# Expert weights in 1 MB transfers of two neighbouring rows per partition, and slot pairs opened oldest first, in a two-layer diffusion transformer with experts

## The chip, the core and the metric

The kernel runs on one core of a Trainium2 chip. The metric is the device time of one execution in microseconds, as the median of several runs.

## What is computed

Two layers over 256 latent and 256 context tokens of width 1024, in float32. Layer 0 mixes the tokens by windowed attention, layer 1 by differential attention; each is followed by a mixture of 32 SwiGLU experts, of which each token uses two. Shift, scale and gate come from a conditioning vector. The part that the change touches, shortened from the reference:

```python
h = rmsnorm(x, norm_g[i, 1]) * (1 + mod[:, 4]) + mod[:, 3]      # mod[:, 3] is the shift
u = xblk @ w_up[e]                                              # w_up[e]: 1024 x 1024
y = (silu(u[:, :512]) * u[:, 512:]) @ w_down[e]                 # w_down[e]: 512 x 1024
out[token] += y * weight[token, e]
```

The experts of layer 0 see all 512 tokens, those of layer 1 the 256 latent ones. Both layers read every expert: 32 x 6.29 MB each, 403 MB of the 484 MB that the kernel reads.

## The kernel before

**Experts.** They are taken in 16 pairs a layer. The two experts of a pair (s = 0, 1) lie side by side in halves of 64 rows or columns, each with room for 64 tokens. For each pair PE gathers the tokens (L1148), transposes them (L1194, in `spread_tokens`, where DVE also adds the shift, L1196), multiplies them with w_up (`up`, L1205: 8 steps of k, 4 matmuls of 128x512 each), ACT and DVE apply the gate (`gate`, L1212 to L1214), PE transposes the result (L1236), multiplies with w_down (`down`, L1248: 4 steps of k), and spreads it back over the tokens (`combine`, L1287). The stages of neighbouring pairs overlap by an order written out by hand: the down matmuls of one pair come right before the up matmuls of the next. The last pair of a layer takes w_down by columns (`down_last`, L1260). A step k uses 128 rows of the weights: k*128 to k*128 + 127, one row on each partition.

**Weights.** All large weights go through one list, `plan`, in a fixed order, by DMAs that SP issues (`Stream.one`, L177), into 43 slots of 4 KB per partition (`Slot`). The list `free` is a queue: a slot that is freed goes to its end and the next use takes its head. A DMA waits until the last reader of its slot is done. Each expert DMA is 512 KB: 128 rows of 4 KB, which follow each other in memory. The same slots hold the split weights and other large values of the attention: `split` (L513, L517) turns a streamed float32 weight into a high and a low part, on ACT and on POOL or DVE, for the projections (L542).

**Around the experts.** `Post` normalizes the tokens after the attention, computes the router's logits and turns the tokens into rows (`flip`; in layer 1 the copies are L921 on ACT). `logit_bias` (L835 to L847) computes what the shift adds to the logits. After the fifth pair a condition decides whether an expert has over 64 tokens; the branch for that isn't taken here (the jump shows at L1081).

```python
        def one(self):                              # Stream
            src, shape = plan[self.pos]
            self.pos += 1
            s = Slot()
            v = s.f(*shape)
            nc.sync.dma_start(v, src)               # L177
            self.ready.append((s, v))
```

Of the kernel before, what the change touches and what calls it, by code (L numbers as in the profile page):

```python
# [18 lines left out]
OP = mybir.AluOpType  # L19
# [37 lines left out]
def _hybrid_dit(ctx, tc, a, out):  # L57
# [5 lines left out]
    places = [[nc.alloc_sbuf_tensor_at(f"slot{c}{i}", [128, 1024], dt, offset=base + 4096 * i).ap()  # L63
               for c, dt in (("f", F32), ("r", F32R))] for i in range(SLOTS)]
    const = ctx.enter_context(tc.tile_pool(name="const", bufs=1))
    pool = ctx.enter_context(tc.tile_pool(name="act", bufs=1))
# [45 lines left out]
    free = list(range(SLOTS))  # L112

    class Slot:
        def __init__(self, recent=False):
            assert free, "no slot left"
            self.s = free.pop(-1 if recent else 0)

# [10 lines left out]
        def free(self):  # L129
            free.append(self.s)  # L130
            self.s = None

    class Ring:
# [29 lines left out]
    class Stream:  # L163
# [23 lines left out]
    def plan_mod(l, third, halves, k):  # L187
        w = a["mod_w"][l, k * 128:(k + 2) * 128]
        for h in halves:
            for q in range(2):  # L190
                c0 = third * 2048 + q * 1024 + h * 512
                plan.append((w[:, c0:c0 + 512].rearrange("(q p) n -> p q n", p=128), (2, 512)))

    def plan_cols(src, c0, ks=range(0, KT, 2)):
        for k in ks:
            plan.append((src[k * 128:(k + 2) * 128, c0:c0 + 512].rearrange("(q p) n -> p q n", p=128), (2, 512)))

    def plan_out(src):
        for n in range(4):
            for k in range(0, KT, 4):  # L200
                plan.append((src[k * 128:(k + 4) * 128, n * 256:(n + 1) * 256].rearrange("(q p) n -> p q n", p=128),
                             (4, 256)))

    def plan_experts(l):
        for p in range(NE // 2):
            for k in range(KT):
                for s in range(2):
                    plan.append((a["moe_w_up"][l, 2 * p + s, k * 128:(k + 1) * 128, :], (1024,)))
            for k in range(4):
                for s in range(2):  # L210
                    w = a["moe_w_down"][l, 2 * p + s]
                    if p + 1 < NE // 2:
                        plan.append((w[k * 128:(k + 1) * 128, :], (1024,)))
                    else:
                        plan.append((w[:, k * 256:(k + 1) * 256].rearrange("(q p) n -> p q n", p=128), (4, 256)))

    late_cols = [(c, h, k) for c in (3, 2, 4, 5) for h in range(2) for k in range(0, KT, 2)]

    def plan_late(n):
        for _ in range(n):  # L220
            c, h, k = late_cols.pop(0)
            c0 = c * 1024 + h * 512
            plan.append((a["mod_w"][1, k * 128:(k + 2) * 128, c0:c0 + 512].rearrange("(q p) n -> p q n", p=128),
                         (2, 512)))

    wq0, wq1 = a["win_w_qkv"][0], a["diff_w_qkv"][0]
    mod_steps = [(m // 3, m % 3, (0, 1), k) for m in range(1, 4) for k in range(0, KT, 2)]
    for d in range(4):
        for k in range(0, KT, 4):
            for q in range(2):  # L230
                c0 = q * 1024 + d * 256
                plan.append((a["mod_w"][0, k * 128:(k + 4) * 128, c0:c0 + 256].rearrange("(q p) n -> p q n", p=128),
                             (4, 256)))
        plan_cols(wq0, 1024, (2 * d,))
# [14 lines left out]
    for k in range(KT):  # L249
        plan.append((a["diff_w_o"][0, k * 128:(k + 1) * 128, :], (1024,)))  # L250
    plan_experts(1)
# [178 lines left out]

    x_slots = [Slot(recent=True) for _ in range(KT // 2)]
    xT = [x_slots[k // 2].f(2, 512)[:, k % 2] for k in range(KT)]
# [400 lines left out]
    v0s.free()  # L833

    def logit_bias(l, nr):  # L835
        ps = bank("G")
        for k in range(KT):
# [11 lines left out]
    def part(v, c0, nt, n):  # L849
        return v[:, c0:c0 + nt * n].rearrange("p (t n) -> p t n", t=nt)  # L850

    class Post:
        def __init__(self, l, nt, lb=None):
# [5 lines left out]
            if nr == 2:  # L859
# [3 lines left out]
                for h in range(2):  # L863
# [5 lines left out]
                    pe.matmul(ps, ones, dg, start=True, stop=True)  # L869
                    se.activation(self.db.f()[:, h * 512:(h + 1) * 512], ps, AF.Copy)  # L870
            self.norm = Norm(self.T, 2 if nr == 2 else 4, ge, tags="s" if nr == 2 else "st")
# [5 lines left out]
            homes[l].slot.free()  # L877
            self.slots = [[Slot() for _ in range(1 if t in WHOLE[l] else 2)] for t in range(nt)]
            self.tok = [[s.r() if len(g) > 1 else s.f() for s in g] for g in self.slots]
# [6 lines left out]
        def scaled(self, k):  # L886
            l = self.l
            if k % 4 == 0:
                self.xs[k // 4] = [Slot() for _ in range(2)]
            xa = self.xs[k // 4][k % 4 // 2].f(2, 512)[:, k % 2, :self.T]  # L890
# [16 lines left out]
        def flip(self, h, tags, ks=range(4)):  # L907
            for t in range(self.nt):
                if ks[0] == 0:
                    self.banks[t] = bank(tags[t])  # L910
                ps = self.banks[t]
                for k in ks:
                    pe.transpose(ps[:, k * 128:(k + 1) * 128], self.xa[4 * h + k][:, t * 128:(t + 1) * 128], ident)
                cs = slice(ks[0] * 128, (ks[-1] + 1) * 128)
                hs = slice(h * 512 + ks[0] * 128, h * 512 + (ks[-1] + 1) * 128)
                if t < 2 and len(self.tok[t]) > 1:
                    hi, lo = (v[:, hs] for v in self.tok[t])
                    se.activation(hi, ps[:, cs], AF.Copy)
                    ve.tensor_tensor(lo, ps[:, cs], hi.bitcast(F32), op=OP.subtract)
                elif self.nr == 1:  # L920
                    se.activation(self.slots[t][-1].f()[:, hs], ps[:, cs], AF.Copy, scale=self.ri[:, t:t + 1])  # L921
                elif t % 2 == 0:
                    se.activation(self.slots[t][-1].f()[:, hs], ps[:, cs], AF.Copy)
                else:
                    ve.tensor_copy(self.slots[t][-1].f()[:, hs], ps[:, cs])
            if ks[-1] == 3:
# [51 lines left out]
    def moe(l, nt, post, after, finish):  # L978
# [77 lines left out]
        for p in range(np_):  # L1056
# [17 lines left out]
            if p == IF_AT:  # L1074
# [116 lines left out]
    def spread_tokens(l, st, h):  # L1191
        ps = bank("G")
        for k in range(4):
            pe.transpose(ps[:, k * 128:(k + 1) * 128], st["x"][h][:, k * 128:(k + 1) * 128], ident)  # L1194
        o = row("t")
        ve.tensor_tensor(o.rearrange("p (k c) -> p k c", k=4), ps.rearrange("p (k c) -> p k c", k=4),  # L1196
                         mods[l][:, 3, 4 * h:4 * h + 4, 0:1].to_broadcast([128, 4, 128]), op=OP.add)
        st["xt"].append(o)

    def up(st, u, k):  # L1200
        w = [stream.next() for _ in range(2)]
        for h in range(2):
            for s in range(2):
                c0 = (k % 4) * 128 + 64 * s
                pe.matmul(u[h][64 * s:64 * s + 64, :], st["xt"][k // 4][:, c0:c0 + 64],  # L1205
                          w[s][1][:, h * 512:(h + 1) * 512], start=(k == 0), stop=(k == KT - 1))
        for s in range(2):
# [33 lines left out]
    def down(acT):  # L1241
        y = [bank("B"), bank("B")]
        for k in range(4):
            w = [stream.next() for _ in range(2)]
            for h in range(2):
                for s in range(2):
                    c0 = k * 128 + 64 * s
                    pe.matmul(y[h][64 * s:64 * s + 64, :], acT[:, c0:c0 + 64],  # L1248
                              w[s][1][:, h * 512:(h + 1) * 512], start=(k == 0), stop=(k == 3))
            for s in range(2):  # L1250
                w[s][0].free()
        return y
# [41 lines left out]
    def overflow(l, nt, key, W, ri, tok, hT):  # L1294
        T = nt * 128
        for t in range(nt):
            for h in range(2):
# [13 lines left out]
                for k in range(4):  # L1311
                    ve.tensor_scalar(hT[4 * h + k][:, t * 128:(t + 1) * 128], ps[:, k * 128:(k + 1) * 128],
                                     mods[l][:, 3, 4 * h + k, 0:1], None, op0=OP.add)
        Wov = row("p", (128, nt, NE))
# [5 lines left out]
        with tc.For_i(0, NE, 1) as i:  # L1320
# [12 lines left out]
            ve.tensor_copy(wrow[:, :T], ps[:, :T])  # L1333
            wu = a["moe_w_up"][l, bass.ds(i, 1)].rearrange("o (k p) n -> p (o k) n", p=128)
            wd = a["moe_w_down"][l, bass.ds(i, 1)].rearrange("o (k p) n -> p (o k) n", p=128)
# [178 lines left out]
    def move_x(after):  # L1514
        slots = [Slot() for _ in range(2)]
        with tc.issue_after(after.ins):
# [270 lines left out]
```

## Time and profile before

| | before |
|---|---|
| median of 3 runs | 1559.56 us (1555.63 to 1561.87) |
| profiled execution | 1559.65 us |
| its span | 1557.9 us |
| granted TensorE clock, mean | 0.974 of 2.4 GHz |
| PE busy | 1459.4 us, 94% |
| DVE, ACT, POOL busy | 44%, 25%, 12% |
| moved by SP's queue | 483.66 MB |

The page counts the busy time of each engine over one profiled execution. PE's matmuls overlap, so a busy PE need not be at its peak; what ends its idle time is told by the views of waits. The kernel has four stretches: layer 0's attention (0 to about 300 us), its experts (to 800), layer 1's attention (to 1065), its experts (to about 1535), and a short end.

### The profile page before, as it was taken

The page shows a single profiled execution, that of the slowest core. Times are in us where ns is not written, and L with a number is a line of the kernel's source. Part 1 is how long each engine was busy: PE and PEld are TensorE (multiplying, and loading weights), DVE is VectorE, ACT ScalarE, POOL GpSimd, SP SyncE. Part 2 cuts the span into 40 slices and gives each one's busy share as a digit, 9 for nine tenths or more (in the row PEclk, how much of TensorE's full clock was granted, in tenths as well). Part 3 has the DMA queues.
Part 4 walks back from the last instruction along what each step waited for, and adds up shares of the span by engine and source line. Part 5 has one row for each costly group of instructions (what it writes and reads, how often), then busy time and mean ns, then how long its engine had stood idle before and what let it go on. Part 6 is the DMA issues. An engine that isn't in the chain of part 4 may idle for free. (4 is left out here: it accounts for less than half of the span.)

```text
span 1557.9 us, 20210 instructions
## 1 busy us (share of the span) xinstructions
PE 1459.4 (94%) x7407; PEld 802.0 (51%) x7407; DVE 692.2 (44%) x1617; ACT 385.2 (25%) x823; POOL 186.2 (12%) x147
## 2 busy tenths in 40 slices
PE   6998999799999999999997889798999899999997
PEld 4765567444444454445445578684434343443444
DVE  3348862533333343334348976863223232332333
ACT  4426652211100111001123236552111110110112
POOL 2314541000000000000014364100000000000000
PEclk9999999799999999999997999998999999999999
DMA  9777225799989999999963842477999999999992
GB/s 329 245 230 250 82 96 194 281 373 399 390 348 393 399 398 386 402 399 399 381 210 95 287 168 81 167 272 279 388 409 409 408 409 409 409 409 409 409 396 73
DMA packets 169696, 485.67 MB, mean 312 GB/s; under 512 B 20826, under 2 KB 41587, under 8 KB 169587
## 3 DMA queue, kind: packets, MB, share of 16 engines
q1 hardware_dynamic: 169088, 483.66, 81.9%
q8 instruction: 63, 1.03, 0.3%
q10 hardware_dynamic: 498, 0.60, 0.1%
q14 instruction: 47, 0.38, 0.1%
HBM read 483.16 MB, written 1.05 MB: 311 GB/s over the span
## 5 line engine op out<-in xcount | busy, mean ns | idle before, releaser
L1205 PE MATMUL ps<-slotf,row 128*64 128x512 f32 x2048 | 450.8, 595 | 2.1 <-DVE row L1196 2.1
L1205 PEld LDWEIGHTS ps<-slotf,row 128*64 128x64 f32 x2048 | 145.6, 137 | 291.1 <-issue 275.3
L1248 PE MATMUL ps<-slotf,row 128*64 128x512 f32 x960 | 212.6, 595 | 0.0
L542 PE MATMUL ps<-slotr,slotr 128*128 128x512 f32 x768 | 193.6, 405 | 9.5 <-DVE slotf L1410 4.2
L505 DVE SCALAR_TENSOR_TENSOR slotf<-ps,mod,slotf 128x256 f32<-128x256 f32 x408 | 167.3, 476 | 62.4 <-PE ps L1287 29.7
L542 PEld LDWEIGHTS ps<-slotr,slotr 128*128 128x128 f32 x768 | 145.1, 194 | 48.2 <-DVE slotf L1410 5.0
L1248 PEld LDWEIGHTS ps<-slotf,row 128*64 128x64 f32 x960 | 66.2, 137 | 124.9 <-issue 118.1
L1213 DVE SCALAR_TENSOR_TENSOR row<-row,ps 128x512 f32<-128x512 f32 x30 | 20.6, 688 | 234.4 <-ACT row L1212 234.4
L1212 ACT ACTIVATE row<-ps 128x512 f32<-128x512 f32 x30 | 17.9, 597 | 427.8 <-PE ps L1205 388.4
L1274 DVE SCALAR_TENSOR_TENSOR row<-ps,ty,row 128x512 fp32r<-128x512 f32 x60 | 45.1, 751 | 176.4 <-ACT row L1273 173.2
L1273 ACT ACTIVATE row<-ps,ty 128x512 fp32r<-128x512 f32 x60 | 41.3, 688 | 262.9 <-PE ps L1248 262.6
L1287 PE MATMUL ps<-row,row 128*128 128x512 f32 (+1 forms) x512 | 104.5, 349 | 1.1 <-DVE slotf L505 1.0
L1287 PEld LDWEIGHTS ps<-row,row 128*128 128x128 f32 x512 | 77.3, 189 | 36.6 <-ACT row L1212 21.1
L517 POOL TENSOR_TENSOR slotr<-slotf,slotr 128x1024 fp32r<-128x1024 f32 x32 | 81.0, 2543 | 90.0 <-ACT slotr L513 62.0
L1196 DVE TENSOR_TENSOR row<-ps,mod 128x512 f32<-128x512 f32 x64 | 42.7, 687 | 102.4 <-PE ps L1194 101.7
L477 POOL TENSOR_TENSOR row<-row,row 128x512 f32<-128x512 f32 (+1 forms) x13 | 15.0, 1157 | 576.0 <-PE ps L1287 519.9
L1148 PE MATMUL ps<-slotf,row 128*128 128x512 f32 x128 | 65.3, 634 | 6.9 <-PEq L1081 4.7
L1148 PE MATMUL ps<-slotr,row 128*128 128x512 f32 x256 | 70.6, 420 | 0.0
L513 ACT ACTIVATE slotr<-slotf 128x1024 fp32r<-128x1024 f32 x44 | 46.0, 1056 | 49.3 <-DMA slotf<-in_diff_w_qkv 22.9
L1148 PEld LDWEIGHTS ps<-slotr,row 128*128 128x128 f32 x256 | 48.1, 198 | 10.0 <-issue 0.8
L1509 DVE SCALAR_TENSOR_TENSOR row<-slotf,keep,row 128x512 f32<-128x512 f32 x42 | 50.6, 1222 | 1.1
L1373 PE MATMUL ps<-slotr,slotr 128*128 128x512 f32 x192 | 47.6, 399 | 0.0
(311 smaller groups left out, 1552.2 us busy)
## 6 DMA issues: line engine op xcount, KB each, us to landing
slotf<-in_moe_w_up SPq DMA_DIRECT2D x512, 512.0 KB, 9.5
slotf<-in_moe_w_down SPq DMA_DIRECT2D x256, 512.0 KB, 10.1
slotf<-in_mod_w SPq DMA_DIRECT2D x96, 512.0 KB, 6.0
slotf<-in_diff_w_qkv SPq DMA_DIRECT2D x24, 512.0 KB, 4.4
slotf<-in_win_w_qkv SPq DMA_DIRECT2D x12, 512.0 KB, 5.1
slotf<-in_win_w_o SPq DMA_DIRECT2D x8, 512.0 KB, 4.1
slotf<-in_diff_w_o SPq DMA_DIRECT2D x8, 512.0 KB, 4.4
slotf<-in_x SPq DMA_DIRECT2D x2, 512.0 KB, 4.0
```

Of the source, the lines that this page charges most:

```text
L505: ve.scalar_tensor_tensor(xT[k][:, sl], ps[:, sl], g[:, k, r:r + 1], xT[k][:, sl], op0=OP.mult, op1=OP.add)
L513: se.activation(hv, v, AF.Copy)
L517: (eng or (ge if split_i[0] % 3 == 0 else ve)).tensor_tensor(lv, v, hv.bitcast(F32), op=OP.subtract)
L542: pe.matmul(ps[t], h[:, x, ts], w[y][:, kk, :], start=(k + kk == 0 and n == 0), stop=(k + kk == KT - 1 and n == 2))
L1148: pe.matmul(g, P[:, t, :] if len(tok[t]) > 1 else P[:, t, :].bitcast(F32), v[:, hs], start=(t == 0 and i == 0), stop=(t == nt - 1 and i == ...
L1196: ve.tensor_tensor(o.rearrange("p (k c) -> p k c", k=4), ps.rearrange("p (k c) -> p k c", k=4), mods[l][:, 3, 4 * h:4 * h + 4, 0:1].to_bro ...
L1205: pe.matmul(u[h][64 * s:64 * s + 64, :], st["xt"][k // 4][:, c0:c0 + 64], w[s][1][:, h * 512:(h + 1) * 512], start=(k == 0), stop=(k == KT ...
L1248: pe.matmul(y[h][64 * s:64 * s + 64, :], acT[:, c0:c0 + 64], w[s][1][:, h * 512:(h + 1) * 512], start=(k == 0), stop=(k == 3))
L1274: ve.scalar_tensor_tensor(yl, y[h], wsl, yh.bitcast(F32), op0=OP.mult, op1=OP.subtract)
L1287: pe.matmul(out, part[:, c * 128:(c + 1) * 128], st["PT"][:, :T], start=(i == 0), stop=(i == 1))
L1373: pe.matmul(ps, w[x][:, k % 4, ms], oT0[k][1][:, y, :], start=(k == 0 and i == 0), stop=(k == KT - 1 and i == 2))
L1509: ve.scalar_tensor_tensor(acc, w[:, kk, :], keep[:, k + kk:k + kk + 1], acc, op0=OP.mult, op1=OP.add)
```

## The change

**What it does.** All expert weights except the last pair's w_down of each layer come in DMAs of 1 MB: two neighbouring rows, 8 KB, on each partition, into two neighbouring slots (`Wide`). For that, partition p holds the rows 8p to 8p + 7 of w_up and 4p to 4p + 3 of w_down, so that the rows which one DMA reads lie 32 KB (w_up) and 16 KB (w_down) apart, and step k uses the rows 8p + k (4p + k).

The tokens' columns and the gate's result have to be in the same order. `flip` deals the tokens' columns out by their remainder (`deal`, `dealt`), `gate` writes its result with a stride of 128 columns, and `turned_shift`, new in `logit_bias`, brings the shift into that order once a layer, with two instructions on PE and five on DVE.

A pair of slots is free when both are; `whole_pairs` lists the free pairs, the one that has been free longest first. Single users take one half of such a pair and keep the other for the next of their kind (`spare`), users of two slots take a pair (`buddies`).

The diff, cut:

```diff
+    def whole_pairs():
+        at = {i: n for n, i in enumerate(free)}
+        found = [(max(at[i], at[i + 1]), i) for i in range(0, SLOTS - 1, 2) if i in at and i + 1 in at]
+        return [i for _, i in sorted(found)]
...
     class Slot:
-        def __init__(self, recent=False):
-            assert free, "no slot left"
-            self.s = free.pop(-1 if recent else 0)
+        def __init__(self, recent=False, at=None, kind=""):
+            if at is None:
+                assert free, "no slot left"
+                at = spare.pop(kind, None)
+                if recent:
+                    at = next((i for i in free[::-1] if i ^ 1 not in free), free[-1])
+                elif at not in free:
+                    pairs = whole_pairs()
+                    if pairs:
+                        at = pairs[0]
+                        spare[kind] = at + 1
+                    else:
+                        at = free[0]
+            free.remove(at)
+            self.s = at
...
+    class Wide:
+        def __init__(self):
+            self.at = whole_pairs()[0]
+            free.remove(self.at)
+            free.remove(self.at + 1)
...
+        def free(self):
+            free.extend((self.at, self.at + 1))
...
-            src, shape = plan[self.pos]
+            src, shape, wide = plan[self.pos]
             self.pos += 1
-            s = Slot()
+            s = Wide() if wide else Slot(kind="stream")
             v = s.f(*shape)
-            nc.sync.dma_start(v, src)
+            nc.sync.dma_start(wide_places[s.at // 2] if wide else v, src)
...
     def plan_experts(l):
         for p in range(NE // 2):
-            for k in range(KT):
+            for j in range(KT // 2):
                 for s in range(2):
-                    plan.append((a["moe_w_up"][l, 2 * p + s, k * 128:(k + 1) * 128, :], (1024,)))
...
+                    w = a["moe_w_up"][l, 2 * p + s].rearrange("(p k) n -> p (k n)", k=KT)
+                    plan.append((w[:, j * 2048:(j + 1) * 2048], (2, 1024), True))
+            if p + 1 < NE // 2:
+                for j in range(2):
+                    for s in range(2):
+                        w = a["moe_w_down"][l, 2 * p + s].rearrange("(p k) n -> p (k n)", k=4)
+                        plan.append((w[:, j * 2048:(j + 1) * 2048], (2, 1024), True))
...
-        hi, lo = Slot(), Slot()
+        hi, lo = buddies()
...
+    def turned_shift(l):
+        work = row("x")
+        mod16 = homes[l].v[:, 964:980]
+        ve.tensor_reduce(mod16, ident.rearrange("p (k a) -> p a k", a=16), axis=AX.X, op=OP.add)
+        row8, t = work[:, 0:128], work[:, 128:256].rearrange("p (b a) -> p b a", b=8)
+        ps = bank("G")
+        pe.transpose(ps[0:8, 0:128], mods[l][:, 3, :, 0], ident)
+        ve.tensor_copy(row8[0:8], ps[0:8, 0:128])
+        ps = bank("G")
+        each = work[0:8, 256:384]
+        ve.tensor_copy(each.rearrange("j (k a) -> j k a", k=8), ident[0:8, 0:8].unsqueeze(2).to_broadcast([8, 8, 16]))
+        pe.matmul(ps[:, 0:128], each, row8[0:8], start=True, stop=True)
+        ve.tensor_tensor(t, ps[:, 0:128].rearrange("p (a b) -> p b a", b=8), mod16[:, None, :].to_broadcast([128, 8, 16]),
+                         op=OP.mult)
...
+        ve.tensor_reduce(moe_shift[l], t, axis=AX.X, op=OP.add)
...
+    def dealt(v, k0, n):
+        return v.rearrange("t (b m) -> t b m", b=8)[:, :, 16 * k0:16 * (k0 + n)]
+
+    def deal(v):
+        return v.rearrange("t (m b) -> t b m", b=8)
...
-                    se.activation(self.slots[t][-1].f()[:, hs], ps[:, cs], AF.Copy, scale=self.ri[:, t:t + 1])
+                    se.activation(raw, src, AF.Copy, scale=self.ri[:, t:t + 1])
...
-                stream.ahead(len(free) - 1)
+                stream.ahead(len(stream.ready) + len(whole_pairs()))
...
-        w = [stream.next() for _ in range(2)]
+        if k % 2 == 0:
+            st["w_up"] = [stream.next() for _ in range(2)]
+        w = st["w_up"]
...
-        for s in range(2):
-            w[s][0].free()
+        if k % 2:
+            for s in range(2):
+                w[s][0].free()
...
-        ve.scalar_tensor_tensor(ac, th, 1.0, u[0], op0=OP.add, op1=OP.mult)
-        ve.scalar_tensor_tensor(ac, ac, 0.5, u[1], op0=OP.mult, op1=OP.mult)
+        ve.scalar_tensor_tensor(th, th, 1.0, u[0], op0=OP.add, op1=OP.mult)
+        ve.scalar_tensor_tensor(ac.rearrange("s (k p) -> s p k", k=4), th.rearrange("s (p k) -> s p k", k=4), 0.5,
+                                u[1].rearrange("s (p k) -> s p k", k=4), op0=OP.mult, op1=OP.mult)
```

**Where instructions move.** On SP, at the change from layer 1's attention to its experts. Before, the queue has the last weights of the attention (in_diff_w_o) mixed with the first w_up:

```order
L177 DMA slotf_99<-in_diff_w_o 128x1024
L177 DMA slotf_77<-in_diff_w_o 128x1024
L177 DMA slotf_97<-in_moe_w_up 128x1024
L177 DMA slotf_135<-in_diff_w_o 128x1024
L177 DMA slotf_111<-in_moe_w_up 128x1024
L177 DMA slotf_91<-in_diff_w_o 128x1024
L177 DMA slotf_63<-in_diff_w_o 128x1024
L177 DMA slotf_81<-in_diff_w_o 128x1024
L177 DMA slotf_65<-in_moe_w_up 128x1024
L177 DMA slotf_125<-in_moe_w_up 128x1024
L177 DMA slotf_67<-in_moe_w_up 128x1024
L177 DMA slotf_99<-in_moe_w_up 128x1024
```

and now:

```order
L216 DMA slotf_119<-in_diff_w_o 128x1024
L216 DMA slotf_97<-in_diff_w_o 128x1024
L216 DMA slotf_95<-in_diff_w_o 128x1024
L216 DMA slotw_149<-in_moe_w_up 128x2048
L216 DMA slotw_143<-in_moe_w_up 128x2048
L216 DMA slotw_161<-in_moe_w_up 128x2048
L216 DMA slotw_147<-in_moe_w_up 128x2048
L216 DMA slotw_155<-in_moe_w_up 128x2048
L216 DMA slotw_152<-in_moe_w_down 128x2048
L216 DMA slotw_159<-in_moe_w_up 128x2048
```

The 512 KB DMAs of one row per partition (128x1024) have become half as many of two (128x2048), and the first of them stands behind the last in_diff_w_o.

On PE, in the attention of layer 1 where `logit_bias` runs (mod is the table of shifts and scales; the 1x36 matmuls are the logits' bias, L838 before, L902 now). Before:

```order
L1580 MATMUL ps_7785<-ident,row_7700 128x128 x4
L1610 MATMUL ps_7791<-ident,slotf_71 128x128 x2
L1560 MATMUL ps_7803<-slotr_94,slotr_108 128x512 x2
L1560 MATMUL ps_7809<-slotr_94,slotr_108 128x512 x2
L838 MATMUL ps_7814<-slotf_117,mod_237 1x36 x8
L844 MATMUL ps_7826<-ty_7823,ident 128x36
L1639 MATMUL ps_7610<-slotf_127,slotf_77 128x256 x2
L1580 MATMUL ps_7832<-ident,slotf_75 128x128 x4
```

and now:

```order
L1660 MATMUL ps_7629<-ident,row_7544 128x128 x4
L1690 MATMUL ps_7635<-ident,slotf_59 128x128 x2
L1640 MATMUL ps_7647<-slotr_138,slotr_82 128x512 x2
L1640 MATMUL ps_7653<-slotr_138,slotr_82 128x512 x2
L887 MATMUL ps_7660<-ident,mod_258 8x128
L892 MATMUL ps_7663<-row_7658 128x128
L902 MATMUL ps_7669<-slotf_61,mod_258 1x36 x8
L908 MATMUL ps_7681<-ty_7678,ident 128x36
L1719 MATMUL ps_7454<-slotf_139,slotf_113 128x256 x2
```

The transpose of the shift (8x128) and the matmul that turns it (128x128) have come in between the projection's matmuls (128x512) and the bias, back to back. In layer 0 the same two stand about a dozen matmuls apart.

## Rows read from the trace of the kernel before

**Rows 1.** The page, busy time of PE and PEld over the whole span (us, share, instructions), and what the DMA engines moved in each of the 40 slices of 38.95 us (GB/s).

```profile
PE 1459.4 (94%) x7407; PEld 802.0 (51%) x7407; DVE 692.2 (44%) x1617; ACT 385.2 (25%) x823; POOL 186.2 (12%) x147
...
GB/s 329 245 230 250 82 96 194 281 373 399 390 348 393 399 398 386 402 399 399 381 210 95 287 168 81 167 272 279 388 409 409 408 409 409 409 409 409 409 396 73
```

**Rows 2.** Busy time of each engine in four stretches: start and end (us), length, each engine's busy us and instructions, granted TensorE clock, share of the DMA engines' time, GB/s. 20:40 is the start of the kernel, 300:800 the experts of layer 0, 800:1065 the attention of layer 1, 1065:1535 its experts.

```profile
20.00:40.00 20.00, 18.44 (x130) 12.87 (x130) 7.41 (x20) 8.92 (x18) 8.29 (x7) 0.91 1.03 330
300.00:800.00 500.00, 493.42 (x2368) 236.60 (x2364) 183.98 (x409) 57.22 (x93) 0.00 (x0) 0.99 0.98 381
800.00:1065.00 265.00, 225.59 (x1146) 178.85 (x1146) 203.10 (x457) 126.46 (x283) 90.30 (x58) 0.94 0.53 184
1065.00:1535.00 470.00, 454.56 (x2159) 192.75 (x2157) 133.31 (x282) 52.33 (x96) 0.00 (x0) 0.99 0.98 387
```

**Rows 3.** The chain of work that ended last, in order of time: start us, us, what. From the down matmuls (L1248) of one pair of layer 1 to those of the next, and the down matmuls of the last pair (L1260).

```profile
1247.92 7.02 PE ps L1248 x32
1254.93 13.73 PE ps L1205 x64
...
1277.11 7.02 PE ps L1248 x32
...
1535.10 3.67 PE ps L1260 x32
...
1543.22 1.88 PE ps L1260 x16
```

**Rows 4.** What PE waited for between 1080 and 1535 us: us in total, times, the longest. These are all its rows.

```profile
PE ps L1194 <- DVE row L1152: 6.7, 15, 0.4
PE ps L1148 <- PEq L1081: 4.7, 1, 4.7
PE ps L1205 <- DVE row L1196: 0.5, 1, 0.5
```

**Rows 5.** The DMA queue of SP in order of time (start us, us, engine, line, operation, out<-in, how many merged): the w_up of two neighbouring pairs of layer 1, and the w_down of its last pair.

```profile
1331.08 19.52 SPq L177 DMA_DIRECT2D slotf<-in_moe_w_up  x16
...
1361.78 19.48 SPq L177 DMA_DIRECT2D slotf<-in_moe_w_up  x16
...
1506.46 13.42 SPq L177 DMA_DIRECT2D slotf<-in_moe_w_down  x8
```

**Rows 6.** DMA issues of the page: how many, KB of each, median us from issue to landing.

```profile
slotf<-in_moe_w_up SPq DMA_DIRECT2D x512, 512.0 KB, 9.5
slotf<-in_moe_w_down SPq DMA_DIRECT2D x256, 512.0 KB, 10.1
```

**Rows 7.** PE in order of time: the first down matmuls of two neighbouring pairs of layer 0.

```profile
418.88 1.51 PE L1248 MATMUL ps<-slotf,row 128*64 128x512 f32 x6
...
450.65 1.94 PE L1248 MATMUL ps<-slotf,row 128*64 128x512 f32 x8
```

**Rows 8.** What SP's queue waited for over the whole span, longest first: us in total, times, longest.

```profile
SPq L177 <- DMA slotf<-in_moe_w_up: 304.2, 357, 2.4
```

**Rows 9.** The instructions of two lines of logit_bias: duration in ns (shortest/median/longest), first and last start.

```profile
L840 DVE COPY ty<-ps x2: 176/180/184, 223.3 to 1009.0; 2x36 f32<-2x36 f32 x1, 1x36 f32<-1x36 f32 x1
...
L844 PE MATMUL ps<-ty,ident x6: 274/274/294, 223.8 to 1009.4; 2*128 2x36 f32 x4, 1*128 1x36 f32 x2
```

**Rows 10.** What PE waited for between 800 and 1080 us, the end of layer 0 and the attention of layer 1: us in total, times, longest.

```profile
PE ps L456 <- DVE row L454: 9.1, 1, 9.1
PE ps L542 <- DVE slotf L1410: 4.2, 2, 3.0
PE ps L1476 <- DVE slotf L1509: 3.3, 2, 2.8
PE ps L585 <- POOL slotf L571: 3.1, 1, 3.1
...
PE ps L542 <- DVE row L569: 1.8, 1, 1.8
...
PE ps L844 <- DVE ty L840: 0.9, 1, 0.9
```

**Rows 11.** Durations as in rows 9: L569 (DVE, a strided form: 16 runs of 16 columns), L563 (DVE, plain) and L921 (ACT, the token copies of layer 1).

```profile
L569 DVE TENSOR_TENSOR row<-ps,slotf x28: 280/415/425, 56.1 to 989.3; 128x256 f32<-128x256 f32 x24, 128x128 f32<-128x128 f32 x4
...
L563 DVE TENSOR_TENSOR slotf<-ps,slotf x7: 425/691/693, 55.8 to 987.5; 128x512 f32<-128x512 f32 x6, 128x256 f32<-128x256 f32 x1
...
L921 ACT ACTIVATE slotf<-ps,ri x4: 680/688/697, 1058.8 to 1060.5; 128x512 f32<-128x512 f32 x4
```

**Rows 12.** All engines in order of time around a gate of layer 1: its second DVE step, and the transposes of its result on PE.

```profile
1117.01 0.69 DVE L1214 SCALAR_TENSOR_TENSOR row<-row,ps 128x512 f32<-128x512 f32 x1
...
1120.25 0.60 PE L1236 MATMUL ps<-ident,row 128*128 128x128 f32 x4
```

**Rows 13.** What the engines waited for between 815 and 945 us, longest first.

```profile
POOL slotr L517 <- ACT slotr L513: 29.5, 8, 8.2
ACT slotr L513 <- DMA slotf<-in_diff_w_qkv: 22.9, 12, 5.1
```

**Rows 14.** What SP's queue waited for between 780 and 1060 us, longest first.

```profile
SPq L177 <- PE ps L542: 49.5, 12, 8.0
SPq L177 <- PE ps L1560: 42.9, 5, 22.9
```

More of the change, by code (lines that the diff above doesn't have):

```diff
@@ L64, in _hybrid_dit @@
                for c, dt in (("f", F32), ("r", F32R))] for i in range(SLOTS)]
+    wide_places = [nc.alloc_sbuf_tensor_at(f"slotw{i}", [128, 2048], F32, offset=base + 8192 * i).ap()
+                   for i in range(SLOTS // 2)]
     const = ctx.enter_context(tc.tile_pool(name="const", bufs=1))
@@ L131, in free, with buddies, f @@
             self.s = None
+    def buddies():
+        at = whole_pairs()
+        if not at:
+            return Slot(), Slot()
+        return Slot(at=at[0]), Slot(at=at[0] + 1)
+    class Wide:
[3 more added lines that the diff above has]
+            free.remove(self.at + 1)
+        def f(self, *shape):
+            return wide_places[self.at // 2].rearrange("p (a b) -> p a b", a=shape[0])
+        def free(self):
+            free.extend((self.at, self.at + 1))
     class Ring:
@@ L249, in _hybrid_dit @@
     for k in range(KT):
-        plan.append((a["diff_w_o"][0, k * 128:(k + 1) * 128, :], (1024,)))
+        plan.append((a["diff_w_o"][0, k * 128:(k + 1) * 128, :], (1024,), False))
     plan_experts(1)
@@ L429, in mod_run @@
                 done()
-    x_slots = [Slot(recent=True) for _ in range(KT // 2)]
+    x_slots = [s for _ in range(KT // 4) for s in buddies()]
     xT = [x_slots[k // 2].f(2, 512)[:, k % 2] for k in range(KT)]
@@ L877, in __init__ @@
             homes[l].slot.free()
-            self.slots = [[Slot() for _ in range(1 if t in WHOLE[l] else 2)] for t in range(nt)]
+            if WHOLE[l]:
+                self.slots = [[s] for s in buddies()]
+            else:
+                self.slots = [list(buddies()) for t in range(nt)]
             self.tok = [[s.r() if len(g) > 1 else s.f() for s in g] for g in self.slots]
@@ L888, in scaled @@
             if k % 4 == 0:
-                self.xs[k // 4] = [Slot() for _ in range(2)]
+                self.xs[k // 4] = buddies()
             xa = self.xs[k // 4][k % 4 // 2].f(2, 512)[:, k % 2, :self.T]
@@ L1205, in up @@
                 pe.matmul(u[h][64 * s:64 * s + 64, :], st["xt"][k // 4][:, c0:c0 + 64],
-                          w[s][1][:, h * 512:(h + 1) * 512], start=(k == 0), stop=(k == KT - 1))
-        for s in range(2):
-            w[s][0].free()
+                          w[s][1][:, k % 2, h * 512:(h + 1) * 512], start=(k == 0), stop=(k == KT - 1))
+        if k % 2:
+            for s in range(2):
+                w[s][0].free()
     def gate(u):
@@ L1243, in down @@
         for k in range(4):
-            w = [stream.next() for _ in range(2)]
+            if k % 2 == 0:
+                w = [stream.next() for _ in range(2)]
             for h in range(2):
@@ L1248, in down @@
                     pe.matmul(y[h][64 * s:64 * s + 64, :], acT[:, c0:c0 + 64],
-                              w[s][1][:, h * 512:(h + 1) * 512], start=(k == 0), stop=(k == 3))
-            for s in range(2):
-                w[s][0].free()
+                              w[s][1][:, k % 2, h * 512:(h + 1) * 512], start=(k == 0), stop=(k == 3))
+            if k % 2:
+                for s in range(2):
+                    w[s][0].free()
         return y
@@ L1514, in move_x @@
     def move_x(after):
-        slots = [Slot() for _ in range(2)]
+        slots = buddies()
         with tc.issue_after(after.ins):
```

48 lines of the change are left out of this document (26 added, 22 removed).

## The prediction

> **What bounds the kernel now.** I read the page first, then the stretches, the chain, and last the waits of each engine. TensorE is busy 94% of the span, and the GB/s line shows the weight stream flat at 408 to 409 for nine slices from 1130 us on, and at 396 in the tenth [rows 1]: two resources are near their limits, and the views after it decide which one sets the end. The stretches say where it can matter [rows 2]: in the two expert stages PE is busy 493.4 of 500 us and 454.6 of 470, in the attention of layer 1 (800 to 1065) only 225.6 of 265. The chain through a pair of layer 1 is matmul after matmul with no step that is a DMA [rows 3]: from the first L1248 at 1247.92 to the next at 1277.11 are 29.19 us, and 64 of its up matmuls in 13.73 us are 214.5 ns each. The waits of PE from 1080 to 1535 are 6.7 us on a DVE copy, 4.7 us on the jump at L1081 and 0.5 us more; no weight DMA is among them [rows 4]. So expert weights arrive before they are wanted, and a faster stream has nothing to shorten there.
>
> How much before? A pair is 24 DMAs of 512 KB, 12.58 MB. In layer 1 PE eats that in 29.19 us (431 GB/s), while the queue starts one pair's w_up at 1331.08 and the next at 1361.78, 30.7 us (410 GB/s) [rows 5]: the stream is slower than its user there and lives on its lead. At the end the lead is still this: the last eight w_down start to issue at 1506.46 [rows 5], land 10.1 us later in the median [rows 6], by 1516.6, and their first matmul is at 1535.10 [rows 3]: 18.5 us spare. The last of them is issued at about 1519.9, lands by about 1530, and is wanted near 1543 [rows 3]: 13 us. I take 16 as the margin. In layer 0 a pair lasts 31.77 us (418.88 to 450.65) [rows 7], so PE wants 396 GB/s.
>
> **The change, part by part.** *DMAs.* 512 w_up and 256 w_down DMAs of 512 KB [rows 6] become 256 and 120 of 1 MB and 16 of 512 KB, with the same bytes. SP issues fewer instructions, but what it waits for longest is the landing of earlier transfers, 304.2 us on w_up alone, and slots [rows 8]; issuing is not what holds it. No PE time depends on it: 0. A slot pair comes free after the second of its two rows, so a refill starts up to one row (4 matmuls, 0.86 us) later, against a margin of 16: 0. The price that the trace doesn't show is that of reading 8 KB rows that lie 32 KB apart (16 KB in w_down) where each DMA was one contiguous block. The nearest rows bound it: 409 GB/s, the 4 KB rows now, and 330 GB/s at a DMA share of 1.03, the 1 to 2 KB rows of 20 to 40 us, which lie apart too [rows 2]. I take 409 or a little more, since the packets move away from the small end, and keep both ends for the range.
>
> *Matmuls.* Each up and down matmul moves the same 512 weight columns past the same 64 token columns. Which rows of the weights a k step holds has changed, not their number: 0.
>
> *The turned shift.* Each layer gains a transpose, a matmul and five short DVE operations. The same shape stands in the logit bias: a 1x36 copy of 176 to 184 ns and a matmul of 274 ns [rows 9], for which PE waited 0.9 us [rows 10]. In layer 1 the two new matmuls stand back to back ahead of the logit bias, so PE pays 2 x 0.27 + 0.9 = 1.5 us; in layer 0 a dozen others lie between them, so 0.5 us. Sum +2. Queued behind the waiting matmul are the logit bias and the projection after it; who waits for those is PE itself, so nothing more. Bounds: 0 (if PE was idle there anyway) and +4 (if the copy stands behind a few of DVE's longer operations, the engine being busy 203 of 265 us there [rows 2]).
>
> *Dealt tokens and the strided gate.* Token copies write runs of 64 columns and the gate writes with a stride of 128. One strided DVE form is in the trace: 415 ns for 128x256 where the plain 128x512 takes 691 [rows 11], no dearer per column once a fixed part is allowed for. So 0. The other bound is a doubling. The gate's second step ends at 1117.70 and PE transposes its result at 1120.25 [rows 12]; 0.69 us more fits in those 2.5 us, so 0 even then. The four token copies of layer 1, 0.69 us each [rows 11], stand in the gap before the dispatch: at most +2.8.
>
> *Slots.* Where in layer 1 PE waits for operands that DVE or POOL make from streamed weights, the list from 800 to 1080 has 4.2, 3.3, 3.1 and 1.8 us [rows 10], together 12.4. Some of it starts at DMAs: ACT waited 22.9 us for qkv weights from 815 to 945, and POOL 29.5 us for ACT [rows 13]. Those DMAs wait for slots, 49.5 us on the projection's matmuls and 42.9 us on L1560 [rows 14]. Pairs that open oldest first should ask for slots that PE left earlier. But in that stretch DVE is the busiest but PE and its chain of splits would be next to wait, so I take a quarter, -3. The 9.1 us behind DVE's row of L454 [rows 10] is no transfer and stays. So do the 4.7 us at the jump [rows 4].
>
> Sum: 1559.65 (profiled execution, span 1557.9 and 1.7 around it; the median of the runs shown is 1559.56, the same) + 2 - 3 = 1558.65, say **1558.5 us**. What a measurement of this kernel can tell from no change is about 0.5%, 7.8 us.
>
> **The rivals.** *Faster: the attention of layer 1 closes up.* If the queue's waits on slots are what makes the splits late, all of the 12.4 us go: 1559.65 - 12.4 = 1547. For it: ACT's 22.9 us behind DMAs and 184 GB/s in a stage whose queue could carry 400 [rows 2]. Against it: POOL and DVE stand between the DMA and PE, and DVE is busy 77% of that stage. Chance 0.2.
>
> *Slower: the rows far apart stream more slowly.* The place is the second half of layer 1, where the queue is saturated for ten slices of 38.95 us [rows 1], 389 us, and the margin at the end is 16 us. At a rate R the stream ends 389 x (409/R - 1) us later, and PE begins to wait where that passes 16, at 393 GB/s, only 4% below now. Halfway to the 330 of the row above, at 370, it is 41 - 16 = 25 us: 1584. At 330 it is 93 - 16 = 77: 1637, and layer 0, which wants 396, would add to both. For it: neighbouring partitions now read addresses an exact power of two apart, and the margin is thin. Against: a DMA still fetches 8 KB at a stretch, and the next DMAs of the same expert read what lies between. The Trainium skill, "DMA: Bandwidth & Descriptors", section "Latency and other measured facts", has a row by which pitches that are large powers of two cost bandwidth (207 GB/s at 512 KiB against 214, 103 at 4 MiB) and calls the mechanism an inference; no transfer in this trace has such a pitch, and the page shows none as small as 32 KB. An estimate from that page: its mildest figure, 207 of 214, would make 396 of the 409 GB/s and leave the sum as it is; its 164 at 2 MiB would make 313, and 389 x 0.307 - 16 = 103 us more. Chance of this rival: 0.18.
>
> *The change does not do what it says,* because no whole pair is free and it falls back on single slots: in the order of the queue all expert DMAs but those of each layer's last w_down are 128x2048, so I give it nothing.
>
> **How the numbers follow.** My case holds 0.62 and the time is its own, 1558.5. Range: the faster rival's 1547 and the slower one's 1584 are the ends; what lies beyond (the far end at 330, or more than the listed waits gained) is well under 2 in 10. The likeliest case alone is 1553.5 (half of the 12.4 gone, the turned shift at its 0) to 1566.5 (+4 and +2.8, nothing gone). Faster by over 0.5%, below 1551.8: 0.2; slower, above 1567.4: 0.18; within: 0.62.
>
> **What would show it.** Right: the pair in layer 1 still takes 29.2 us on the chain, GB/s in the last ten slices at 405 or more, no DMA of the expert weights among PE's waits, and PE's busy time within 3 us of 1459. The turned shift: a wait of about 1 us of PE for its copy. The gain in slots: less than 22.9 us of ACT behind DMAs between 815 and 945, and PE's four waits smaller. Wrong: PE's up or down matmuls waiting for weight DMAs from about 1450 us on, with less than 393 GB/s, or a layer-1 attention over 8 us shorter.

## The result, and the profile after

The changed kernel takes 1567.32 us where the kernel before takes 1559.93 (medians of 18 runs each): a ratio of 1.0052, 95% interval [1.0042, 1.0063], about 8 us slower. Run again beside the experiments it was 1568.05 against 1560.42, 1.0050 [1.0034, 1.0066]. The profile taken with the first set fell in a disturbed execution (granted clock 0.756), so the views below are of the profiled execution of the second set, 1568.8 us.

Where the time lies is read from the starts of the first and last up matmuls of each layer in the two traces:

| stretch, us | before | changed | difference |
|---|---|---|---|
| to the first up matmul of layer 0 | 299.6 | 304.6 | +5.0 |
| experts of layer 0 | 497.3 | 502.9 | +5.6 |
| attention of layer 1 | 272.9 | 271.7 | -1.2 |
| experts of layer 1 | 460.9 | 459.9 | -1.0 |
| the end | 27.2 | 28.1 | +0.9 |

One profile of each is not enough for the first and the third row: the gate-only run of the next section changes nothing ahead of the experts and its first stretch was 302.7. Most of the second row stands in every pair of layer 0: 13 of the 14 steps from one pair to the next are 0.32 us longer, 4.2 us together. The step with the jump (37.58 us before, 38.94 in the change) adds 1.4, but it lies between 36.1 and 38.9 us over the profiles of all the runs below, with no order by the gate.

The page of the changed kernel, as in [rows 1]:

```profile
PE 1460.4 (93%) x7413; PEld 803.2 (51%) x7413; DVE 712.7 (45%) x1627; ACT 384.8 (25%) x823; POOL 187.1 (12%) x147
...
GB/s 327 223 222 222 121 55 215 255 377 397 375 344 379 399 399 398 374 399 392 397 247 95 309 134 108 108 239 342 391 422 421 387 416 420 421 421 421 421 375 28
```

PE's busy time is within 1 us of before, and the stream reaches 416 to 422 GB/s in most slices (one between them has 387) where it stood at 408 to 409. The chain of waits through layer 1, as in [rows 3]:

```profile
1256.20 7.02 PE ps L1327 x32
1263.21 13.73 PE ps L1281 x64
...
1285.38 7.02 PE ps L1327 x32
...
1543.35 3.67 PE ps L1340 x32
```

A pair still takes 29.18 us. SP's queue at the same place, as in [rows 5]:

```profile
1354.64 6.77 SPq L216 DMA_DIRECT2D slotw<-in_moe_w_down  x4
1361.51 22.23 SPq L216 DMA_DIRECT2D slotw<-in_moe_w_up  x8
1383.83 6.77 SPq L216 DMA_DIRECT2D slotw<-in_moe_w_down  x4
```

From one pair's w_down to the next are 29.19 us, PE's own pace, where it was 30.7. The queue's longest waits say the same: they are on PE's release of slots now, where before the longest was on transfers [rows 8].

```profile
SPq L216 <- PE ps L1327: 376.3, 57, 13.3
SPq L216 <- PE ps L1281: 351.7, 117, 8.0
```

So the transfers improved as far as PE lets them, and bought nothing in the expert stages, since PE had never waited for them there: the experts of layer 1 take 459.9 us, and 459.2 to 459.9 in the five kernels below that keep the 512 KB transfers. What PE waited for from 300 to 807 us is the row to look at:

```profile
PE ps L1238 <- DVE ty L1263: 7.4, 13, 0.6
PE ps L1258 <- PEq L1155: 3.2, 1, 3.2
```

L1238 are the transposes of the token selection and L1263 the last of three small copies of the token weights (L1164 and L1189 before); the second row is one wait at the jump. The first row as it was before:

```profile
PE ps L1164 <- DVE ty L1189: 3.7, 13, 0.3
```

It is twice as long, in the same 13 pairs. Now DVE in order of time in one pair of layer 0, before, and the PE instruction behind it:

```profile
411.22 0.48 DVE L505 SCALAR_TENSOR_TENSOR slotf<-ps,mod,slotf 128x256 f32<-128x256 f32 x1 [0.17 <-PE ps L1287]
411.62 0.68 DVE L1214 SCALAR_TENSOR_TENSOR row<-row,ps 128x512 f32<-128x512 f32 x1
412.22 2.83 DVE L505 SCALAR_TENSOR_TENSOR slotf<-ps,mod,slotf 128x256 f32<-128x256 f32 x7
414.96 0.32 DVE L1187 COPY ty<-ps 64x1 f32<-64x1 f32 x2
415.29 0.16 DVE L1189 COPY ty<-ps 128x1 f32<-128x1 f32 x1
...
415.60 0.63 PE L1164 MATMUL ps<-ident,row 128*128 128x128 f32 x4 [0.28 <-DVE ty L1189]
```

and changed:

```profile
384.76 0.48 DVE L549 SCALAR_TENSOR_TENSOR slotf<-ps,mod,slotf 128x256 f32<-128x256 f32 x1 [0.19 <-PE ps L1367]
385.16 1.06 DVE L1291 SCALAR_TENSOR_TENSOR row<-row,ps 128x512 f32<-128x512 f32 x1
386.07 2.81 DVE L549 SCALAR_TENSOR_TENSOR slotf<-ps,mod,slotf 128x256 f32<-128x256 f32 x7
388.80 0.32 DVE L1261 COPY ty<-ps 64x1 f32<-64x1 f32 x2
389.13 0.16 DVE L1263 COPY ty<-ps 128x1 f32<-128x1 f32 x1
...
389.43 0.63 PE L1238 MATMUL ps<-ident,row 128*128 128x128 f32 x4 [0.57 <-DVE ty L1263]
```

The gate's second step (L1214, now L1291) takes 1.06 us for 0.68 (a median of 1067 ns for 686). Behind it DVE has no idle time: seven additions, three copies, and PE at the end of the row. What the step is longer, PE waits longer: 0.57 us for 0.28. The duration holds for all 30 gates. First the step as it was before, then the changed one, with the turned shift's copy and the dealt token copies beside it:

```profile
L1214 DVE SCALAR_TENSOR_TENSOR row<-row,ps x30: 676/686/689, 318.7 to 1502.8; 128x512 f32<-128x512 f32 x30
```

```profile
L1291 DVE SCALAR_TENSOR_TENSOR row<-row,ps x30: 1035/1067/1101, 323.7 to 1511.0; 128x512 f32<-128x512 f32 x30
...
L888 DVE COPY row<-ps x2: 270/274/279, 220.5 to 1017.4; 8x128 f32<-8x128 f32 x2
...
L995 ACT ACTIVATE slotf<-ps,ri x4: 688/688/688, 1071.4 to 1073.9; 128x512 f32<-128x512 f32 x4
```

Last, PE's waits from 800 to 1080, as in [rows 10], and ACT's for the streamed qkv weights (820 to 955), as in [rows 13]:

```profile
PE ps L500 <- DVE row L498: 9.9, 1, 9.9
PE ps L586 <- DVE slotf L1490: 4.0, 1, 4.0
PE ps L1556 <- DVE slotf L1589: 2.7, 1, 2.7
...
PE ps L586 <- issue: 2.4, 1, 2.4
PE ps L629 <- POOL slotf L615: 1.7, 2, 0.9
...
PE ps L892 <- DVE row L888: 1.5, 1, 1.5
```

```profile
ACT slotr L557 <- DMA slotf<-in_diff_w_qkv: 36.1, 7, 9.9
```

The four waits that were 12.4 us are 8.4 (the one on L569's row is gone), but a wait of 2.4 us that the profile can't name and the turned shift's 1.5 us are new, and ACT waits longer for weights, 36.1 us for 22.9. That longer wait goes with the new slots: over the twelve profiles of this section and the next it is 30.9 to 36.1 us in the seven kernels that have them and 15.4 to 30.4 in the five that don't.

### The profile page after: what moved, and what is told of

Same layout as the page of the kernel before. It is cut to its first block, busy times and chain, and to the rows that moved or that the text cites. A ratio compares the mean times of both kernels' runs of the same rounds, so it can differ in the third digit from the quotient of the medians.

```text
span 1868.2 us, 19492 instructions
## 1 busy us (share of the span) xinstructions
PE 1796.9 (96%) x7413; PEld 876.3 (47%) x7413; DVE 698.0 (37%) x1627; ACT 385.4 (21%) x823; POOL 185.4 (10%) x147
## 5 line engine op out<-in xcount | busy, mean ns | idle before, releaser
L1281 PE MATMUL ps<-slotw,row 128*64 128x512 f32 x2048 | 575.4, 730 | 2.1 <-DVE row L1270 2.1
L1281 PEld LDWEIGHTS ps<-slotw,row 128*64 128x64 f32 x2048 | 154.0, 150 | 404.0 <-issue 400.7
L1327 PE MATMUL ps<-slotw,row 128*64 128x512 f32 x960 | 270.4, 731 | 0.0
L586 PE MATMUL ps<-slotr,slotr 128*128 128x512 f32 x768 | 231.7, 465 | 4.6 <-ACT slotr L1519 1.7
L586 PEld LDWEIGHTS ps<-slotr,slotr 128*128 128x128 f32 x768 | 152.7, 203 | 71.4 <-issue 6.8
L1327 PEld LDWEIGHTS ps<-slotw,row 128*64 128x64 f32 x960 | 70.2, 149 | 173.1 <-issue 171.4
L1367 PE MATMUL ps<-row,row 128*128 128x512 f32 (+1 forms) x512 | 121.0, 388 | 0.9 <-DVE slotf L549 0.9
L1367 PEld LDWEIGHTS ps<-row,row 128*128 128x128 f32 x512 | 84.9, 207 | 49.7 <-ACT row L1289 27.1
L1270 DVE TENSOR_TENSOR row<-ps,shift 128x512 f32<-128x512 f32 x64 | 42.7, 686 | 136.8 <-PE ps L1268 135.4
L1222 PE MATMUL ps<-slotr,row 128*128 128x512 f32 x256 | 83.0, 478 | 0.0
L1222 PE MATMUL ps<-slotf,row 128*128 128x512 f32 x128 | 76.4, 729 | 5.3 <-PEq L1155 4.5
L1453 PE MATMUL ps<-slotr,slotr 128*128 128x512 f32 x192 | 59.4, 473 | 0.0
L1268 PE MATMUL ps<-ident,row 128*128 128x128 f32 x256 | 43.4, 310 | 6.9 <-DVE row L1226 6.2
```

Source lines behind the costliest of these rows:

```text
L586: pe.matmul(ps[t], h[:, x, ts], w[y][:, kk, :], start=(k + kk == 0 and n == 0), stop=(k + kk == KT - 1 and n == 2))
L1222: pe.matmul(g, P[:, t, :] if len(tok[t]) > 1 else P[:, t, :].bitcast(F32), v[:, hs], start=(t == 0 and i == 0), stop=(t == nt - 1 and i == ...
L1327: pe.matmul(y[h][64 * s:64 * s + 64, :], acT[:, c0:c0 + 64], w[s][1][:, k % 2, h * 512:(h + 1) * 512], start=(k == 0), stop=(k == 3))
L1367: pe.matmul(out, part[:, c * 128:(c + 1) * 128], st["PT"][:, :T], start=(i == 0), stop=(i == 1))
L1453: pe.matmul(ps, w[x][:, k % 4, ms], oT0[k][1][:, y, :], start=(k == 0 and i == 0), stop=(k == KT - 1 and i == 2))
```

## The experiments

The theory is that the strided gate costs what the pairs of layer 0 show, some 4.2 us (0.32 us in 13 steps from pair to pair), and the turned shift the next part. The rivals: the slot order, the rows far apart, the 1 MB transfers, the dealt copies. Ratios are to the kernel before, run on the same chip.

**The change again, and its parts.** These four runs were made before the gate was suspected, to divide the change.

> The changed kernel again, beside the others. The page-by-stretch view should tell where its 8 us (ratio 1.0052) lie: in the two expert stages, if the rows 32 KB apart stream more slowly and PE waits for weights there (GB/s in the last ten slices below 393); around the router and the dispatch of each layer and in PE's waits on DVE, if the turned shift and the dealt copies are what costs; in the two attentions, if the slot order makes weights or splits late.

> The kernel before with the new order of slots alone (pairs free longest first, users of two slots take a pair); DMAs stay 512 KB, rows, tokens and gate as before. If the slot order costs the 8 us: about 1.005 of before. If the rows or the dealt tokens do: within 0.998 to 1.001. My forecast of a small gain from slots would be 0.998.

```diff
+    def whole_pairs():
...
+    def buddies():
...
-            s = Slot()
+            s = Slot(kind="stream")
...
-        hi, lo = Slot(), Slot()
+        hi, lo = buddies()
...
```

> The kernel before with the new row order alone: 512 KB DMAs whose 128 rows of 4 KB lie 32 KB (16 KB) apart, dealt tokens, strided gate, turned shift; slots as before. If dealing and turning cost the 8 us, or rows that lie apart stream more slowly: about 1.005. If the slots or the 1 MB DMAs do: within 0.999 to 1.002. Should rows apart cost bandwidth, GB/s in the last ten slices falls below 393 and PE waits for weights from about 1450 us on.

```diff
-                    plan.append((a["moe_w_up"][l, 2 * p + s, k * 128:(k + 1) * 128, :], (1024,)))
+                    w = a["moe_w_up"][l, 2 * p + s].rearrange("(p k) n -> p k n", k=KT)
+                    plan.append((w[:, k], (1024,)))
...
+        turned_shift(l)
...
```

> The changed kernel with the old row order: 1 MB DMAs of two pieces of 4 KB per partition, new slots, but tokens not dealt, gate not strided, no turned shift. If the dealing and turning cost the 8 us: 1.000 or a little below. If the 1 MB DMAs or the slots do: about 1.005.

```diff
-                    w = a["moe_w_up"][l, 2 * p + s].rearrange("(p k) n -> p (k n)", k=KT)
-                    plan.append((w[:, j * 2048:(j + 1) * 2048], (2, 1024), True))
+                    w = a["moe_w_up"][l, 2 * p + s, j * 256:(j + 1) * 256, :].rearrange("(q p) n -> p q n", p=128)
+                    plan.append((w, (2, 1024), True))
...
-        turned_shift(l)
...
```

Measured: slots alone 1562.07 us, 1.0016 [1.0006, 1.0025]; rows alone 1566.09, 1.0048 [1.0034, 1.0062]; 1 MB with the old rows 1557.57, 0.9990 [0.9978, 1.0002]. Nearly all of the loss comes with the row order and what it drags along. The slots alone cost a little, where I had forecast a gain. Rows of 4 KB that lie 32 KB apart cost no bandwidth; the rows-only kernel and the 1 MB one from 1300 to 1500 us:

```profile
1300.00:1500.00 200.00, 196.25 (x948) 84.30 (x946) 62.60 (x126) 23.34 (x42) 0.00 (x0) 1.00 1.03 409
```

```profile
1300.00:1500.00 200.00, 196.78 (x950) 83.45 (x950) 58.47 (x122) 22.19 (x40) 0.00 (x0) 1.00 1.03 409
```

Both stay at 409 GB/s (last column). Above that are only kernels with 8 KB rows, as the change with its 421.

**The gate, taken away and added by itself.**

> The changed kernel with w_down back in its old rows (1 MB DMAs of two 4 KB pieces) and the gate's result written plainly; w_up rows, dealt tokens, turned shift and slots as changed. Gate theory (the strided second step takes 1067 ns for 684, holds up the weight copies behind it on DVE, and PE's transposes of layer 0 wait for those 0.57 us for 0.28 in 13 pairs): a pair of layer 0 back to 31.77 us, PE's wait back to 3.7 us, 4 to 5 us less than the change, ratio to before about 1.002. Rival (rows, dealing or turned shift cost it): pairs stay at 32.08 us, ratio 1.005.

```diff
-                        w = a["moe_w_down"][l, 2 * p + s].rearrange("(p k) n -> p (k n)", k=4)
-                        plan.append((w[:, j * 2048:(j + 1) * 2048], (2, 1024), True))
+                        w = a["moe_w_down"][l, 2 * p + s, j * 256:(j + 1) * 256, :].rearrange("(q p) n -> p q n", p=128)
+                        plan.append((w, (2, 1024), True))
...
-        ve.scalar_tensor_tensor(th, th, 1.0, u[0], op0=OP.add, op1=OP.mult)
-        ve.scalar_tensor_tensor(ac.rearrange("s (k p) -> s p k", k=4), th.rearrange("s (p k) -> s p k", k=4), 0.5,
-                                u[1].rearrange("s (p k) -> s p k", k=4), op0=OP.mult, op1=OP.mult)
+        ve.scalar_tensor_tensor(ac, th, 1.0, u[0], op0=OP.add, op1=OP.mult)
+        ve.scalar_tensor_tensor(ac, ac, 0.5, u[1], op0=OP.mult, op1=OP.mult)
```

> The kernel before with only w_down's rows 4p + k (512 KB DMAs) and the strided gate. Gate theory: layer 0's pair goes from 31.77 to 32.08 us, layer 1's stays at 29.18, PE's wait for the weight copies from 3.7 to 7.4 us, ratio 1.003. Rival: 1.000.

```diff
-                        plan.append((w[k * 128:(k + 1) * 128, :], (1024,)))
+                        plan.append((w.rearrange("(p k) n -> p k n", k=4)[:, k], (1024,)))
...
+        ve.scalar_tensor_tensor(ac.rearrange("s (k p) -> s p k", k=4), th.rearrange("s (p k) -> s p k", k=4), 0.5,
+                                u[1].rearrange("s (p k) -> s p k", k=4), op0=OP.mult, op1=OP.mult)
```

Measured: the plain gate 1560.86 us, 1.0010 [1.0001, 1.0019], 6 us under the change; the strided gate added to the kernel before 1561.25, 1.0013 [1.0004, 1.0023], 2 us over it. PE's wait in layer 0 does in both what the theory says, and in both profiles it is the first row from 300 to 800 us. The plain gate:

```profile
PE ps L1238 <- DVE ty L1263: 3.6, 13, 0.3
```

The strided gate alone:

```profile
PE ps L1164 <- DVE ty L1189: 7.6, 13, 0.6
```

The starts of neighbouring pairs are 31.79 us apart in the first and 32.06 in the second, against 31.77 before and 32.09 in the change; in layer 1 they are 29.18 to 29.19 in all four. So the longer step does lengthen the wait and the pair. Its price in the total is less certain. Added to the kernel before it costs 2.0 us [0.6, 3.6], under the ratio of 1.003 that was expected; taken away it gives 6 us, with an interval of some 3 us to either side. The 4.2 us of the pairs lie between.

**The turned shift alone.**

> The kernel before with the turned shift computed in both layers and not used. If it is what is left of the cost beside the gate: one wait of PE of about 1.5 us in layer 1 and up to 1 in layer 0, 2 to 3 us in all, ratio 1.0015 to 1.002. If it is hidden: 1.000.

```diff
+    def turned_shift(l):
...
     def logit_bias(l, nr):
+        turned_shift(l)
```

Measured: 1562.71 us, 1.0019 [1.0010, 1.0028], 3 us. Its wait on PE in layer 1:

```profile
PE ps L848 <- DVE row L844: 1.5, 1, 1.5
```

**The waiting taken away, the gate left as it is.** The gate stays strided; only the three small copies behind it change their engine.

> The changed kernel, strided gate and all, with the three small copies of the token weights moved from DVE to ACT, which is idle there. Gate theory: the gate still takes 1067 ns but nothing that PE waits for stands behind it, so PE's wait in layer 0 goes and its pair falls to about 31.5 us, some 8 us under the change, ratio to before 0.9995. Rival (the longer gate is not what PE waits for): no change, 1.005.

```diff
-            ve.tensor_copy(st["w"][pb, 0:1], wps[pb, s:s + 1])
+            se.activation(st["w"][pb, 0:1], wps[pb, s:s + 1], AF.Copy)
...
-            ve.tensor_copy(st["w"][:, 1:2], wps[:, 2:3])
+            se.activation(st["w"][:, 1:2], wps[:, 2:3], AF.Copy)
```

Measured: 1557.70 us, 0.9997 [0.9988, 1.0006], 8 us under the change. The same place in the pair:

```profile
384.96 1.06 DVE L1291 SCALAR_TENSOR_TENSOR row<-row,ps 128x512 f32<-128x512 f32 x1
385.88 2.80 DVE L549 SCALAR_TENSOR_TENSOR slotf<-ps,mod,slotf 128x256 f32<-128x256 f32 x7
...
386.75 0.34 ACT L1261 ACTIVATE ty<-ps 64x1 f32<-64x1 f32 x2 [3.09 <-PE ps L1258]
387.10 0.17 ACT L1263 ACTIVATE ty<-ps 128x1 f32<-128x1 f32 x1
...
388.51 0.60 PE L1238 MATMUL ps<-ident,row 128*128 128x128 f32 x4
```

The gate takes its 1.06 us as before, the copies are done at 387.3, and the transposes start at 388.51 with no wait. A pair falls to 31.55 us, and PE's wait for the copies is gone; its longest wait from 300 to 807 us is now another, which the kernel before has too (L1184 on L1125):

```profile
PE ps L1258 <- DVE row L1199: 2.9, 1, 2.9
```

With the copies on ACT the strided gate takes 31.55 us a pair and the plain one 31.52 (next runs), where the two were 0.32 us apart with the copies on DVE. This separates the long step (nearly harmless in the pairs) from what was queued behind it (the cost).

**The same move on the two better bases.**

> 1 MB DMAs of two 4 KB pieces in the old rows (no dealing, no turned shift, plain gate), new slots, and the three small copies of the token weights on ACT. If what PE waits for in each pair of layer 0 is the weight copies behind DVE's gate and additions: pair 31.5 us where the same kernel without the move has 31.76, some 4 us less, ratio to before about 0.9965. If those waits only change their name: 0.999.

> The kernel before with only the three small copies on ACT. Same theory: pair of layer 0 at 31.5 us, ratio about 0.9975. Otherwise 1.000.

On each of the two, the edit is the one above. Measured: 1 MB DMAs in the old rows with the copies on ACT 1553.98 us, 0.9954 [0.9939, 0.9968]; the kernel before with the copies on ACT 1555.80, 0.9966 [0.9954, 0.9978]. In both a pair of layer 0 takes 31.52 us, and both beat the kernel before and the change. In the kernel before, the edit gives 5.3 us [3.4, 7.2], of which 0.25 us in 13 pairs make 3.3. One thing stays open: the first of the two lies 6.7 us, give or take 2.7, under the change with the copies on ACT (0.9954 for 0.9997). The turned shift accounts for 3 of them and the pairs for 0.4, and no run tells where the rest lies.

**The turned shift in the changed kernel, and what dealing costs.**

> As the plain-gate run (w_up rows, dealt tokens, new slots, 1 MB DMAs, w_down in old rows), with the turned shift left out, so that the shift is added in the wrong order of columns. If the turned shift costs 3 us in the changed kernel too: ratio to before 0.999, 3 us under the plain-gate run's 1.0010. If dealing the tokens is what is left: 1.001.

```diff
-        turned_shift(l)
+        moe_shift[l] = mods[l][:, 3, :, 0]
```

Measured: 1559.22 us, 0.9992 [0.9981, 1.0002], 2.8 us under the plain-gate run's 1.0010, each against the kernel before on its own chip: the turned shift costs about the same in both places. What then still tells it from the 1 MB kernel with the old rows (0.9990) is w_up's rows and the dealt tokens, so those two together cost nothing that can be told from these intervals of 0.1% to either side.

## Why the prediction was wrong, step by step

**The number.** 1567.32 us lies inside the range of 1547 to 1584, but by luck: the upper end came from rows that stream more slowly, and they don't. The forecast was 1 us faster than before, and the change is 8 us slower. The forecast took 0.5% as the least that can be told from no change; the intervals here are about 0.1% to either side, so the loss is clear.

**What bounds the kernel: right.** PE bounds it, the pair of layer 1 kept its 29.18 us, PE's busy time changed by 1 us, and no expert DMA appears among its waits. A stream that is 3% faster was worth nothing in the expert stages, as forecast.

**Rows far apart: right, and the slower rival is dead.** 4 KB rows 32 KB apart gave 409 GB/s, as contiguous ones do, and 8 KB rows gave 421. The Trainium skill, "DMA: Bandwidth & Descriptors", section "Latency and other measured facts", has bandwidth fall at pitches that are large powers of two, 512 KiB and more; nothing of the kind shows at 32 KB here, a pitch that it doesn't list. The result is slower by another way than the one that I gave 0.18.

**The strided gate: this is the step that failed.** I priced it at 0, with 0 at the far bound too: "0.69 us more fits in those 2.5 us, so 0 even then". Measured, it is 4.2 us by the pairs (2 to 6 by the totals). Two things were wrong in it. The size: I took a doubling as the far bound and zero as likely, because one strided DVE form [rows 11] is no dearer; but that form moves runs of 16 columns, and the gate writes single columns 512 bytes apart, which cost 0.38 us of 0.69. The Trainium skill, "SBUF — State Buffer", section "Door 1: The DMA port swizzle", says that each access that crosses to a new 16-byte line of SBUF pays a penalty. The trace agrees in direction (1067 ns for 686), though no run here shows that the line is the reason; the page was the warning that I didn't use. The place: I looked for who reads the gate's result, found slack in a pair of layer 1, and stopped. I did not ask what is queued behind the gate on DVE in a pair of layer 0. There, PE already waited 0.28 us in 13 pairs for the last copy of that queue, so the slack was below zero before anything was added. The row L1164 on L1189 stands first in PE's waits of layer 0; I showed that view for layer 1 alone [rows 4].

**The turned shift: right.** +2 forecast with bounds 0 and +4; 3.0 us [1.6, 4.4] measured by itself and 2.8 in the changed kernel. The 8x128 copy takes 274 ns where I took 180, and the wait in layer 1 is 1.5 us for 0.9.

**Dealt tokens: right.** The ACT copies take 688 ns before and after.

**Slots: the second term that failed.** I forecast -3; alone they cost 2.5 us [0.9, 3.9]. The four waits did shrink by 4 us in the changed kernel's profile, as the faster rival wanted, but a new wait of 2.4 us stands beside them, and ACT waits 13 us longer for its weights, where I had named a shorter wait as the sign of the gain. Over the profiles of all twelve kernels the first stretch takes 302.4 to 304.9 us with the new slots and 299.6 to 303.2 without, layer 1's attention 265.7 to 272.3 with them and 272.1 to 275.3 without. So there may be a gain where I looked for it, and a loss in the first stretch, which I didn't look at. That is not shown: each kernel has one profile, and the granted clock in layer 1's attention lies between 0.91 and 0.94 from profile to profile. Which of the slot rules does it stays open too.

**The sum.** Gate 4.2 (by the pairs), turned shift 3.0, slots 2.5, dealing about 0. The 1 MB transfers were not run without the new slots. The two kernels with the new slots and the old rows, 0.9990 with 1 MB and 1.0016 with 512 KB, differ by 4 us in favour of 1 MB, and their intervals don't meet; where those 4 us come from, no run shows. That makes 6 of the 8 us. The remaining 2 lie within the uncertainty of the five terms and are not explained further; the gate's 2 to 6 us are the widest of them.

## What to carry to other kernels

Price a longer instruction by the engine's queue, not by its own reader: list what stands behind it up to the next instruction that another engine waits for, in every stage, and start from the waits that exist already, however short. A wait of 0.28 us that repeats in 13 pairs is a place with no slack; taking it away by moving three small copies made even the kernel before 5.3 us faster. When a resource is not what the bounding engine waits for, its improvement is worth nothing there, and what the new layout costs elsewhere decides.

## What the runs showed of the hardware

- DVE's SCALAR_TENSOR_TENSOR of 128x512 takes 686 ns (median) with a plain result and 1067 ns when it is written one column every 512 bytes; ACT's copy that writes runs of 64 columns, read with a stride of 8 from PSUM, takes 688 ns, as the plain one.
- The rate of the stream went by the length of the row and not by the size of the DMA: 4 KB rows gave 409 GB/s in 512 KB transfers (next to each other or 32 KB apart) and in 1 MB transfers; 8 KB rows gave 421, with the queue by then waiting for PE's slots, so that their own ceiling isn't seen.
